# Batched fp32 matmul on one core: all 32 batches in one TensorE loop, the first pair's x loaded in fp32 and rounded on chip

## The chip, the cores and the metric

The kernel runs on one core of one Trainium2 chip. The metric is the device time of one execution in microseconds. The kernel before takes 513.82 us, the median of 3 runs (513.75 to 513.89). A second number comes from one profiled execution, which took 514.01 us and from which all the durations below are read.

## What is computed

For each of 32 batches, out = x @ weight, with x of 512 x 1024, weight of 1024 x 768 and out of 512 x 768, all fp32 in memory. The reference is one line:

```python
return np.matmul(x, weight).astype(np.float32)   # x [32, 512, 1024], weight [32, 1024, 768]
```

The kernels round x and weight to bf16 on the way in and accumulate in fp32.

## The kernel before

Five engines run programs written out by hand, tied together by semaphores; nothing is scheduled by a planner.

**Loads.** GpSimd (POOL, `on_pool`, L309) issues the loads on its own DMA queue, q0 in the profile. These DMAs read fp32 and write bf16, so the rounding costs no engine anything. A batch's weight (3.15 MB in memory) goes to one of four slots `ws` (`load_w`, L89), after the batch that used the slot four batches earlier has been multiplied. x is loaded for two batches in one DMA (`load_x`, L94, 4.19 MB in memory) into one of two slots `xs`, after the transposes of the pair that used the slot. In it partitions 0 to 63 hold the first batch of the pair and 64 to 127 the second, eight rows of 1024 in each partition. Only batch 0's x comes in fp32, by one DMA that SyncE (SP) issues on queue q1 at the very start (L359), into memory that a later output tile uses.

**Pairs.** Batch 0 stands alone, then come 15 pairs (1, 2), (3, 4) to (29, 30), and batch 31 stands alone again. For a pair TensorE (`pair_on_pe`, L159) waits for x, transposes it in 8 groups of 4 instructions (`transpose`, L151), two bf16 numbers travelling as one fp32 word, and then multiplies the two batches, each after a wait for its weight (`take(s_wr)`, L168; the wait itself is L157). VectorE spreads each transposed group from PSUM into `both` (L233). Batch 0 needs 32 transposes for itself because its x is fp32, batch 31 needs 16. Seven turns of a loop hold 14 of the pairs; the rest is written out.

**Results.** ScalarE and VectorE copy the products out of PSUM into `outs` (L265, L268, L279, L281). Outputs are paired as (0, 1), (2, 3) and so on: a tile holds the first batch in partitions 0 to 63 and the second in 64 to 127, so a copy covers 64 partitions. Batches 30 and 31 are the exception: each has a tile of 128 partitions (`one` for batch 30) and copies of 128 partitions (L276, and L265 and L268 in that form).

**Stores.** A pair's 3.15 MB goes out in one DMA (`store`, L107). POOL issues stores 0 to 10 between its loads, and stores 11, 12 and 13 behind the last load. SP first waits in order for every weight to land (`landed`, L304, which passes the news to TensorE), and then issues the first half of batch 30, store 14, the second half of batch 30 and both halves of batch 31 (`store_half`, L111). A half of a batch is 0.79 MB, 128 partitions x 6144 B.

**What orders the work.** Each queue's DMAs start in the order in which they were issued, and POOL and SP each wait at the head of their own list. So a load whose slot is free can stand behind a wait of another load.

Of the kernel before, what the change touches and what calls it, by code (L numbers as in the profile page):

```python
# [12 lines left out]
def kernel(  # L13
# [16 lines left out]
    AHEAD = 3  # L30
    LATE = 4
    HELD = 4
    GROUPS = 2 * MT
    W_SLOTS, X_SLOTS, OUT_SLOTS = 4, 2, 4
    LOOPS = (B - 4) // W_SLOTS
    LOOPED = 2 * LOOPS

# [3 lines left out]
    x_view = x.rearrange("b (mi mo) k -> b mi mo k", mi=P)  # L41
    pair_view = x[1:B - 1].rearrange("(p r) (mi mo) k -> p (r mi) mo k", r=2, mo=2 * MT)
    out_view = out.rearrange("b (mi mo) n -> b mi (mo n)", mi=P)
# [9 lines left out]
    outs = [sbuf(f"out{i}", [P, 2 * ROW], F32) for i in range(OUT_SLOTS)]  # L53
    one = sbuf("one", [P, ROW], F32)
    x_first = outs[3][:, :MT * K].rearrange("p (mo k) -> p mo k", mo=MT)
# [11 lines left out]
    s_first, s_zero, s_ident = sem("s_first"), sem("s_zero"), sem("s_ident")  # L67
# [13 lines left out]
    def pt_done(k):  # L81
        return GROUPS * (k + 2)

    def out_done(b):
        return 2 * (b + 1)
# [8 lines left out]
    def load_x(k):  # L94
        if k >= X_SLOTS:
            pool.wait_ge(s_pt, pt_done(k - X_SLOTS))
        slot = xs[k % X_SLOTS]
        if 2 * k + 1 == B - 1:
            pool.dma_start(out=slot[:, :MT], in_=x_view[B - 1]).then_inc(s_x[k % X_SLOTS], 16)
        else:  # L100
            pool.dma_start(out=slot, in_=pair_view[k]).then_inc(s_x[k % X_SLOTS], 16)  # L101
# [5 lines left out]
    def store(eng, a, sem):  # L107
        copied(eng, out_done(2 * a + 1) - 1)
        eng.dma_start(out=two_view[a], in_=outs[a % OUT_SLOTS]).then_inc(sem, 16)  # L109

    def store_half(b, p):  # L111
        src = one if b == B - 2 else outs[(b // 2) % OUT_SLOTS]
        half = slice(p * N2, (p + 1) * N2)
        copied(sp, 2 * b + p)
        sp.dma_start(out=out_view[b, :, half], in_=src[:, half]).then_inc(s_fin, 16)
# [3 lines left out]
    def stationary(b, mt):  # L119
        if b == 0 or b == B - 1:  # L120
            return both[mt][:, 0].rearrange("p j h i r -> p j (h i) r")
        return both[mt][:, (b - 1) % 2].rearrange("p j h i r -> p j (h i) r")
# [20 lines left out]
    def rows_of(b, g):  # L143

        if b == 0:
            return [x_first[:, g // 2, JT * (g % 2) + i::KT] for i in range(JT)]
        words = xs[(b // 2) % X_SLOTS].bitcast(F32)
        mo = g if b == B - 1 else g // 2 + MT * (g % 2)
        return [words[:, mo, j::JT] for j in range(JT)]

    def transpose(b, g):  # L151
        for i, rows in enumerate(rows_of(b, g)):
            last = pe.transpose(pts[g % 2][:, i, :], rows, ident)  # L153
        last.then_inc(s_pt, 1)
# [4 lines left out]
    def pair_on_pe(k, q):  # L159

        b = 2 * k + 1
        take(s_xr)
        for g in range(GROUPS):
            if GROUPS * q + g > 1:
                pe.wait_ge(s_c, GROUPS * q + g - 1)
            transpose(b, g)
        for r in range(2):
            take(s_wr)  # L168
            for mt in range(MT):
                at = 4 * q + 2 * r + mt // 2  # L170
                if not r:
                    pe.wait_ge(s_c, GROUPS * q + 2 * mt + 2)
                pe.wait_ge(s_a, at + 1 + mt % 2)
                if b + r == B - 2 and mt == MT - 1:
                    pe.wait_ge(s_dp, 2 * (B - 2))
                else:
                    pe.wait_ge(s_d, at + 1 + mt % 2)
                multiply(b + r, mt)

    def on_pe():  # L180
        pe.wait_ge(s_ident, 1)
        pe.wait_ge(s_first, 16)
        for g in range(GROUPS):
            if g > 1:
                pe.wait_ge(s_c, g - 1)
            transpose(0, g)
        pe.wait_ge(s_c, GROUPS).then_inc(s_c, -GROUPS)
        take(s_wr)
        for mt in range(MT):
            multiply(0, mt)  # L190
        with pe.Fori(0, LOOPS):
            for q in range(2):
                pair_on_pe(q, q)
            pe.wait_ge(s_c, 2 * GROUPS).then_inc(s_c, -2 * GROUPS)
            pe.wait_ge(s_a, 9).then_inc(s_a, -8)
            pe.wait_ge(s_d, 9).then_inc(s_d, -8)
        pair_on_pe(LOOPED, 0)
        b = B - 1
        take(s_xr)
        for g in range(MT):  # L200
            pe.wait_ge(s_c, GROUPS + max(g - 1, 0))
            transpose(b, g)
        take(s_wr)
        for mt in range(MT):
            j = 2 * b + mt // 2
            pe.wait_ge(s_c, GROUPS + mt + 1)
            pe.wait_ge(s_ap if mt % 2 else s_a, j - 1 if mt % 2 else 5 + mt // 2)
            pe.wait_ge(s_dp, j - 1)
            multiply(b, mt)
# [3 lines left out]
    def spread_first(g):  # L213
        xT, pt = both[g // 2][:, 0].rearrange("p j h i r -> p j (h i) r"), pts[g % 2]
        for j in range(2):
            last = dve.tensor_copy(  # L216
                xT[:, 2 * (g % 2) + j].rearrange("p (h i) r -> p r h i", h=2),
                pt[:, 2 * j:2 * j + 2].rearrange("p r (i h) -> p r h i", h=2),
            )
        return last  # L220

    def spread_pair(k, g):

        pt = pts[g % 2].bitcast(BF16).rearrange("p j (b i r) -> p j b i r", b=2, r=2)
        tile, half = both[g // 2], g % 2
        if 2 * k + 2 == B - 2:

            rows = tile[:, 1].rearrange("p j h i r -> p j (h i r)").rearrange(
                "p j (m r) -> p j m r", r=2
            )  # L230
            dve.tensor_copy(tile[:, 0, :, half], pt[:, :, 0])  # L231
            return dve.tensor_copy(rows[:, :, half::2, :], pt[:, :, 1])  # L232
        return dve.tensor_copy(tile[:, :, :, half].rearrange("p b j i r -> p j b i r"), pt)  # L233

    def spread_last(g):
        return dve.tensor_copy(  # L236
            both[g][:, 0].rearrange("p j h i r -> p (j h i r)"),
            pts[g % 2].bitcast(BF16).rearrange("p j m -> p (j m)"),
        )

    def slot_free(eng, b):
        a = b // 2
        if a >= OUT_SLOTS and b % 2 == 0 and b < B - 2:
            eng.wait_ge(s_st[a % OUT_SLOTS], 16 * (a // OUT_SLOTS))
        if b == B - 1:
            eng.wait_ge(s_st[a % OUT_SLOTS], 16 * (a // OUT_SLOTS))

    def pieces(b, p, i):

        pm = pms[p][i]  # L250
        if b >= B - 2:
            dst = one if b == B - 2 else outs[(b // 2) % OUT_SLOTS]
            at = p * N2 + 512 * i
            return [(dst[:, at:at + 512], pm)]
# [4 lines left out]
    def out_on_act(b, p):  # L259
        j = 2 * b + p  # L260
        if p == 0:
            slot_free(act, b)
# [7 lines left out]
    def out_on_dve(b, p):  # L270
        j = 2 * b + p
        if p == 0:
            slot_free(dve, b)
        dve.wait_ge(s_mm, 2 * j + 2)
        if b >= B - 2:
            dve.tensor_copy(*pieces(b, p, 1)[0]).then_inc(s_dp, 1)  # L276
            return
# [4 lines left out]

    def on_dve():

        for b in range(B):
            if b == 0 or b % 2:
                spread = {0: spread_first, B - 1: spread_last}.get(b)
                for g in range(MT if b == B - 1 else GROUPS):
                    dve.wait_ge(s_pt, (0 if b == 0 else pt_done(b // 2 - 1)) + g + 1)
                    (spread(g) if spread else spread_pair(b // 2, g)).then_inc(s_c, 1)  # L290
                if b:
                    out_on_dve(b - 1, 1)
            out_on_dve(b, 0)
            if b % 2 or b == B - 1:
                out_on_dve(b, 1)

    def on_act():
        for b in range(B):
            out_on_act(b, 0)
            if b % 2 == 0:  # L300
                landed(act, (s_x, s_xr), b // 2)
            out_on_act(b, 1)

    def landed(eng, what, i):  # L304

        slots, ready = what
        eng.wait_ge(slots[i % len(slots)], 16 * (i // len(slots) + 1)).then_inc(ready, 1)

    def on_pool():  # L309
# [12 lines left out]
        load_x(0)  # L322
        load_w(1)
        load_w(2)
        load_x(1)
        for b in range(B):
            if b % 2 and b + AHEAD + 1 < B:
                load_x((b + AHEAD) // 2)
            a = (b - 5) // 2
            if b % 2 and 0 <= a < B // 2 - 1 - HELD:  # L330
                store(pool, a, s_st[a % OUT_SLOTS])
            if b + AHEAD < B:
                load_w(b + AHEAD)
            if b == B - LATE:
                for a in range(B // 2 - 1 - HELD, B // 2 - 2):
                    store(pool, a, s_st[a % OUT_SLOTS])
# [59 lines left out]
```

## Time and profile before

| What | Value |
|---|---|
| profiled execution | 514.01 us, of which the instructions' span is 512.2 |
| TensorE, busy | 437.9 us; first transpose at 12.41, first matmul at 20.66, last matmul ends 501.3 |
| TensorE granted clock, mean | 0.946 |
| VectorE, ScalarE, busy | 206.8 us, 110.2 us |
| a weight load, from issue to landing | 41.6 us (median of 32) |
| a pair's x, from issue to landing | 30.0 us (median of 15) |
| batch 0's x, from issue to landing | 11.3 us |
| last four half stores, from issue to landing | 9.0 to 13.9 us |

How to read it: the busy time of an engine says how long it worked, not whether it was waited for. The time from issue to landing holds the time for which a transfer stood behind others in its queue. The DMA share of a stretch is the mean busy share of the 16 DMA engines that all queues use; it can come out a little above 1, because packets overlap.

### The profile page before, as it was taken

What the parts mean: (1) busy time and instruction counts of PE and PEld (TensorE: products, weight loads), DVE (VectorE), ACT (ScalarE), POOL (GpSimd) and SP (SyncE); (2) the same over time, 40 slices, a digit from 0 to 9 for tenths busy, and PEclk for the clock granted to TensorE, in tenths of its full rate; (3) what the DMA queues carried; (4) which work ended last, traced back from release to release, by engine and by line L of the source; (5) the groups of instructions that cost most, each with busy time, mean ns of one, the idle gap of its engine ahead of it and who ended that gap; (6) DMA issues with size and microseconds to landing.
All of it is one profiled execution on the core that took longest, in us unless ns stands there. A gap on an engine that the chain in (4) does not pass through costs nothing. (4 is left out here: it accounts for less than half of the span.)

```text
span 512.2 us, 6109 instructions
## 1 busy us (share of the span) xinstructions
PE 437.9 (85%) x2576; PEld 278.8 (54%) x2576; DVE 206.8 (40%) x332; ACT 110.2 (22%) x189; POOL 33.7 (7%) x68
## 2 busy tenths in 40 slices
PE   0899989999795997979989798898969979799991
PEld 0666656666463654636646365464635646456660
DVE  0463543545362352533525245153631615416230
ACT  1013122222211221112221122112122121221210
POOL 3000000101010010100101001010100100100000
PEclk9999999999997998979989899799998989979997
DMA  8999999999999999999999999999999999999996
GB/s 254 214 214 222 222 207 224 213 225 325 220 335 218 240 312 224 333 218 255 297 222 337 218 264 286 219 339 218 288 266 213 341 216 306 250 214 257 432 429 290
DMA packets 9803, 135.40 MB, mean 264 GB/s; under 512 B 1088, under 2 KB 1088, under 8 KB 1600
## 3 DMA queue, kind: packets, MB, share of 16 engines
q0 software_dynamic: 8928, 126.88, 96.3%
q1 hardware_dynamic: 864, 8.39, 4.0%
q8 instruction: 5, 0.08, 0.1%
q14 instruction: 6, 0.05, 0.0%
HBM read 167.77 MB, written 50.33 MB: 426 GB/s over the span
## 5 line engine op out<-in xcount | busy, mean ns | idle before, releaser
L134 PE MATMUL pm<-w,xT 128*128 128x256 bf16 (+1 forms) x2048 | 356.2, 337 | 40.2 <-PEq L157 40.2
L134 PEld LDWEIGHTS pm<-w,xT 128*128 128x128 bf16 x2048 | 205.8, 101 | 186.2 <-issue 61.5
L279 DVE COPY out<-pm 64x512 f32<-64x512 f32 x120 | 82.5, 687 | 198.9 <-PE pm L134 198.1
L265 ACT COPY out<-pm 64x512 f32<-64x512 f32 (+1 forms) x122 | 70.7, 580 | 292.8 <-PE pm L134 292.1
L233 DVE COPY xT<-pt 128x1024 bf16<-128x1024 bf16 x112 | 72.2, 687 | 61.0 <-PE pt L153 61.0
L153 PE MATMUL pt<-ident,x 128*128 128x128 f32 x496 | 80.0, 302 | 10.5 <-DVE xT L233 9.5
L153 PEld LDWEIGHTS pt<-ident,x 128*128 128x128 f32 x496 | 69.2, 209 | 21.8 <-DVE xT L233 17.4
L268 ACT COPY out<-pm 64x512 f32<-64x512 f32 (+1 forms) x62 | 35.8, 578 | 90.0 <-PE pm L134 90.0
L281 DVE COPY out<-pm 64x512 f32<-64x512 f32 x60 | 41.2, 686 | 0.0
L101 POOL DMA_DIRECT2D x<-in_x_dram x15 | 8.0, 532 | 266.6 <-PE pt L153 266.4
L92 POOL DMA_DIRECT2D w<-in_weight_dram x32 | 17.2, 538 | 125.4 <-PE pm L134 124.4
L153 PE MATMUL pt<-ident,out 128*128 128x128 f32 x32 | 6.9, 373 | 12.7 <-DMA out<-in_x_dram 12.4
L153 PEld LDWEIGHTS pt<-ident,out 128*128 128x128 f32 x32 | 5.3, 207 | 14.1 <-issue 12.4
L216 DVE CAST xT<-pt 128x256 bf16<-128x256 f32 x16 | 6.0, 441 | 14.4 <-PE pt L153 14.1
L109 POOL DMA_DIRECT2D out_dram<-out x14 | 7.5, 536 | 1.2 <-DVE out L281 0.7
L231 DVE COPY xT<-pt 128x512 bf16<-128x512 bf16 x8 | 3.4, 420 | 4.1 <-PE pt L153 4.1
L276 DVE COPY out<-pm 128x512 f32<-128x512 f32 x2 | 1.4, 692 | 8.4 <-PE pm L134 8.4
L236 DVE COPY xT<-pt 128x1024 bf16<-128x1024 bf16 x4 | 2.6, 688 | 5.2 <-PE pt L153 5.2
L232 DVE COPY xT<-pt 128x512 bf16<-128x512 bf16 x8 | 3.3, 416 | 0.0
L276 DVE COPY one<-pm 128x512 f32<-128x512 f32 x2 | 1.4, 687 | 3.2 <-PE pm L134 3.2
L265 ACT COPY one<-pm 128x512 f32<-128x512 f32 x2 | 1.2, 585 | 4.0 <-PE pm L134 4.0
L268 ACT COPY one<-pm 128x512 f32<-128x512 f32 x2 | 1.2, 586 | 4.0 <-PE pm L134 4.0
(8 smaller groups left out, 2.7 us busy)
## 6 DMA issues: line engine op xcount, KB each, us to landing
w<-in_weight_dram POOLq DMA_DIRECT2D x32, 1536.0 KB, 41.6
out_dram<-out POOLq DMA_DIRECT2D x14, 3072.0 KB, 36.9
x<-in_x_dram POOLq DMA_DIRECT2D x15, 2048.0 KB, 30.0
out_dram<-out SPq DMA_DIRECT2D x1, 3072.0 KB, 19.9
out<-in_x_dram SPq DMA_DIRECT2D x1, 2048.0 KB, 11.3
out_dram<-one SPq DMA_DIRECT2D x2, 768.0 KB, 13.4
out_dram<-out SPq DMA_DIRECT2D x2, 768.0 KB, 10.0
x<-in_x_dram POOLq DMA_DIRECT2D x1, 1024.0 KB, 25.3
```

The lines of the kernel that those rows point to most:

```text
L92: pool.dma_start(out=ws[b % W_SLOTS], in_=w_view[b]).then_inc(s_w[b % W_SLOTS], 16)
L101: pool.dma_start(out=slot, in_=pair_view[k]).then_inc(s_x[k % X_SLOTS], 16)
L109: eng.dma_start(out=two_view[a], in_=outs[a % OUT_SLOTS]).then_inc(sem, 16)
L134: last = pe.matmul(pm[bank][:, at:at + size], xT[:, ko // 2, :, ko % 2], w[:, ko, off:off + size], start=(ko == 0), stop=(ko == KT - 1),)
L153: last = pe.transpose(pts[g % 2][:, i, :], rows, ident)
L216: last = dve.tensor_copy(xT[:, 2 * (g % 2) + j].rearrange("p (h i) r -> p r h i", h=2), pt[:, 2 * j:2 * j + 2].rearrange("p r (i h) -> p r ...
L231: dve.tensor_copy(tile[:, 0, :, half], pt[:, :, 0])
L233: return dve.tensor_copy(tile[:, :, :, half].rearrange("p b j i r -> p j b i r"), pt)
L265: last = act.copy(*piece)
L268: act.copy(*pieces(b, p, 2)[0]).then_inc(s_ap, 1)
L279: last = dve.tensor_copy(*piece)
L281: dve.tensor_copy(*pieces(b, p, 2)[1]).then_inc(s_dp, 1)
```

## The change

The pairs become (0, 1), (2, 3) to (30, 31), for x as they already were for out. TensorE's whole program is one loop of eight turns with two pairs each; the separate code for batch 0 and batch 31, the tile `one` and the spreads in two parts go away.

The x of the first pair is loaded in fp32 by SP into memory of output tiles 2 and 3 (32 KB in each partition). VectorE rounds four of its eight rows into the first x slot and ScalarE the other four, ScalarE's last one after all of VectorE's; then ScalarE tells TensorE that x is ready. POOL's list at the start becomes weights 0 and 1, x of the second pair, weights 2 and 3. After that its order in a pair is as before: x of two pairs ahead, a store, two weights. The weights are now those of the batches that use the slots just freed by this pair's own two batches. Stores 0 to 11 stand between the loads, 12 and 13 behind them.

The last pair's output tile is in the pair layout, too. SP issues store 14 first and then four halves: the first two come out of partitions 0 to 63 (batch 30), the last two out of partitions 64 to 127 (batch 31), each as two pieces of 6144 B in a partition.

```diff
-    LOOPS = (B - 4) // W_SLOTS
+    LOOPS = B // W_SLOTS
...
-    x_view = x.rearrange("b (mi mo) k -> b mi mo k", mi=P)
-    pair_view = x[1:B - 1].rearrange("(p r) (mi mo) k -> p (r mi) mo k", r=2, mo=2 * MT)
-    out_view = out.rearrange("b (mi mo) n -> b mi (mo n)", mi=P)
+    x_view = x.rearrange("(p r) (mi mo) k -> p (r mi) mo k", r=2, mo=2 * MT)
...
-    x_first = outs[3][:, :MT * K].rearrange("p (mo k) -> p mo k", mo=MT)
+    x_first = all_outs[:, 4 * ROW:4 * ROW + 2 * MT * K].rearrange("p (mo k) -> p mo k", mo=2 * MT)
...
     def store_half(b, p):
-        src = one if b == B - 2 else outs[(b // 2) % OUT_SLOTS]
+        a, r = divmod(b, 2)
+        rows = slice(H * r, H * (r + 1))
         half = slice(p * N2, (p + 1) * N2)
+        src, dst = (
+            t[rows].rearrange("i (h c) -> i h c", h=2)[:, :, half]
+            for t in (outs[a % OUT_SLOTS], two_view[a])
+        )
         copied(sp, 2 * b + p)
-        sp.dma_start(out=out_view[b, :, half], in_=src[:, half]).then_inc(s_fin, 16)
+        sp.dma_start(out=dst, in_=src).then_inc(s_fin, 16)
...
     def on_pe():
         pe.wait_ge(s_ident, 1)
...
         with pe.Fori(0, LOOPS):
-            for q in range(2):
-                pair_on_pe(q, q)
...
-        pair_on_pe(LOOPED, 0)
...
+            for k in range(2):
+                pair_on_pe(k)
...
+    def cast_first(eng, copy, rows):
+
+        eng.wait_ge(s_first, 16)
+        for mo in rows:
+            if mo == 2 * MT - 1:
+                eng.wait_ge(s_cast, 1)
+            last = copy(xs[0][:, mo], x_first[:, mo])
+        return last
+
     def on_dve():
...
+        dve.sem_inc(s_d, 2)
+        cast_first(dve, dve.tensor_copy, range(MT)).then_inc(s_cast, 1)
...
     def on_act():
+        act.sem_inc(s_a, 2)
+        cast_first(act, act.copy, range(MT, 2 * MT)).then_inc(s_xr, 1)
...
-        load_x(0)
         load_w(1)
+        load_x(1)
         load_w(2)
-        load_x(1)
...
+        load_w(3)
+        for k in range(PAIRS - 2):
+            load_x(k + 2)
+            if k >= 2:
+                store(pool, k - 2, s_st[(k - 2) % OUT_SLOTS])
+            load_w(2 * k + 4)
+            load_w(2 * k + 5)
+        for a in range(PAIRS - 2 - HELD, PAIRS - 2):
+            store(pool, a, s_st[a % OUT_SLOTS])
...
-        store_half(B - 2, 0)
-        store(sp, B // 2 - 2, s_fin)
-        store_half(B - 2, 1)
-        store_half(B - 1, 0)
-        store_half(B - 1, 1)
+        store(sp, PAIRS - 2, s_fin)
+        for b in (B - 2, B - 1):
+            for p in range(2):
+                store_half(b, p)
```

More of the change, by code (lines that the diff above doesn't have):

```diff
@@ L29 @@
     ROW = MT * N
-    AHEAD = 3
-    LATE = 4
-    HELD = 4
+    PAIRS = B // 2
+    HELD = 2
     GROUPS = 2 * MT
     W_SLOTS, X_SLOTS, OUT_SLOTS = 4, 2, 4
-    LOOPS = (B - 4) // W_SLOTS
-    LOOPED = 2 * LOOPS
+    LOOPS = B // W_SLOTS
     pe, dve, act, pool, sp = nc.tensor, nc.vector, nc.scalar, nc.gpsimd, nc.sync
     w_view = weight.rearrange("b (ki ko) n -> b ki ko n", ki=P)
-    x_view = x.rearrange("b (mi mo) k -> b mi mo k", mi=P)
-    pair_view = x[1:B - 1].rearrange("(p r) (mi mo) k -> p (r mi) mo k", r=2, mo=2 * MT)
-    out_view = out.rearrange("b (mi mo) n -> b mi (mo n)", mi=P)
+    x_view = x.rearrange("(p r) (mi mo) k -> p (r mi) mo k", r=2, mo=2 * MT)
     two_view = out.rearrange("(p r) (i m) n -> p (r i) (m n)", r=2, m=2 * MT)
@@ L52 @@
     both = [sbuf(f"xT{i}", [P, 2, JT, 2, H, 2], BF16) for i in range(MT)]
-    outs = [sbuf(f"out{i}", [P, 2 * ROW], F32) for i in range(OUT_SLOTS)]
-    one = sbuf("one", [P, ROW], F32)
-    x_first = outs[3][:, :MT * K].rearrange("p (mo k) -> p mo k", mo=MT)
+    all_outs = sbuf("outs", [P, OUT_SLOTS * 2 * ROW], F32)
+    outs = [all_outs[:, i * 2 * ROW:(i + 1) * 2 * ROW] for i in range(OUT_SLOTS)]
+    x_first = all_outs[:, 4 * ROW:4 * ROW + 2 * MT * K].rearrange("p (mo k) -> p mo k", mo=2 * MT)
     pts = [nc.alloc_psum_tensor(f"pt{i}", [P, JT, P], F32).ap() for i in range(2)]
@@ L65, in sem @@
         return sems[-1]
-    s_first, s_zero, s_ident = sem("s_first"), sem("s_zero"), sem("s_ident")
+    s_first, s_cast, s_zero, s_ident = (sem(f"s_{n}") for n in ("first", "cast", "zero", "ident"))
     s_w = [sem(f"s_w{i}") for i in range(W_SLOTS)]
@@ L81, in pt_done @@
     def pt_done(k):
-        return GROUPS * (k + 2)
-    def out_done(b):
-        return 2 * (b + 1)
+        return GROUPS * (k + 1)
     def load_w(b):
@@ L96, in load_x @@
             pool.wait_ge(s_pt, pt_done(k - X_SLOTS))
[L97 to L101, printed above, removed]
+        pool.dma_start(out=xs[k % X_SLOTS], in_=x_view[k]).then_inc(s_x[k % X_SLOTS], 16)
     def copied(eng, j):
@@ L107, in store @@
     def store(eng, a, sem):
-        copied(eng, out_done(2 * a + 1) - 1)
+        copied(eng, 4 * a + 3)
         eng.dma_start(out=two_view[a], in_=outs[a % OUT_SLOTS]).then_inc(sem, 16)
     def store_half(b, p):
-        src = one if b == B - 2 else outs[(b // 2) % OUT_SLOTS]
+        a, r = divmod(b, 2)
+        rows = slice(H * r, H * (r + 1))
         half = slice(p * N2, (p + 1) * N2)
+        src, dst = (
+            t[rows].rearrange("i (h c) -> i h c", h=2)[:, :, half]
+            for t in (outs[a % OUT_SLOTS], two_view[a])
+        )
         copied(sp, 2 * b + p)
-        sp.dma_start(out=out_view[b, :, half], in_=src[:, half]).then_inc(s_fin, 16)
+        sp.dma_start(out=dst, in_=src).then_inc(s_fin, 16)
     def stationary(b, mt):
-        if b == 0 or b == B - 1:
-            return both[mt][:, 0].rearrange("p j h i r -> p j (h i) r")
-        return both[mt][:, (b - 1) % 2].rearrange("p j h i r -> p j (h i) r")
+        return both[mt][:, b % 2].rearrange("p j h i r -> p j (h i) r")
     SPLITS = (
@@ L141, in multiply, with transpose @@
         last.then_inc(s_mm, 1)
[L143 to L153, printed above, removed]
+    def transpose(k, g):
+        words = xs[k % X_SLOTS].bitcast(F32)
+        mo = g // 2 + MT * (g % 2)
+        for j in range(JT):
+            last = pe.transpose(pts[g % 2][:, j, :], words[:, mo, j::JT], ident)
         last.then_inc(s_pt, 1)
@@ L157, in take, with await_copies, pair_on_pe @@
         pe.wait_ge(s, 1).then_inc(s, -1)
-    def pair_on_pe(k, q):
-        b = 2 * k + 1
+    def await_copies(s, n, last, step):
+        wait = pe.wait_ge(s, n)
+        if n == last:
+            wait.then_inc(s, -step)
+    def pair_on_pe(k):
         take(s_xr)
         for g in range(GROUPS):
[L164 to L167, printed above, removed]
+            if GROUPS * k + g > 1:
+                pe.wait_ge(s_c, GROUPS * k + g - 1)
+            transpose(k, g)
+        for b in (2 * k, 2 * k + 1):
@@ L168, in pair_on_pe @@
             take(s_wr)
             for mt in range(MT):
[L170 to L178, printed above, removed]
+                if b % 2 == 0:
+                    await_copies(s_c, GROUPS * k + 2 * mt + 2, 2 * GROUPS, 2 * GROUPS)
@@ L180, in on_pe @@
+                at = 2 * b + mt // 2 + 1 + mt % 2
+                await_copies(s_a, at, 9, 8)
+                await_copies(s_d, at, 9, 8)
+                multiply(b, mt)
     def on_pe():
         pe.wait_ge(s_ident, 1)
[L182 to L190, printed above, removed]
@@ L191, in on_pe @@
-        with pe.Fori(0, LOOPS):
-            for q in range(2):
-                pair_on_pe(q, q)
-            pe.wait_ge(s_c, 2 * GROUPS).then_inc(s_c, -2 * GROUPS)
-            pe.wait_ge(s_a, 9).then_inc(s_a, -8)
-            pe.wait_ge(s_d, 9).then_inc(s_d, -8)
-        pair_on_pe(LOOPED, 0)
[L198 to L209, printed above, removed]
@@ L213, in spread_first @@
[L213 to L222, printed above, removed]
-        pt = pts[g % 2].bitcast(BF16).rearrange("p j (b i r) -> p j b i r", b=2, r=2)
[L225 to L245, printed above, removed]
+        with pe.Fori(0, LOOPS):
+            for k in range(2):
+                pair_on_pe(k)
+    def spread(k, g):
+        pt = pts[g % 2].bitcast(BF16).rearrange("p j (b i r) -> p j b i r", b=2, r=2)
+        to = both[g // 2][:, :, :, g % 2].rearrange("p b j i r -> p j b i r")
+        return dve.tensor_copy(to, pt)
@@ L246, in slot_free @@
+    def slot_free(eng, a):
+        if a >= OUT_SLOTS:
             eng.wait_ge(s_st[a % OUT_SLOTS], 16 * (a // OUT_SLOTS))
@@ L250, in pieces @@
         pm = pms[p][i]
[L251 to L254, printed above, removed]
         mine = outs[(b // 2) % OUT_SLOTS][H * (b % 2):H * (b % 2 + 1)]
@@ L260, in out_on_act @@
         j = 2 * b + p
-        if p == 0:
-            slot_free(act, b)
+        if b % 2 == 0 and p == 0:
+            slot_free(act, b // 2)
         act.wait_ge(s_mm, 2 * j + 1)
@@ L271, in out_on_dve @@
         j = 2 * b + p
-        if p == 0:
-            slot_free(dve, b)
+        if b % 2 == 0 and p == 0:
+            slot_free(dve, b // 2)
         dve.wait_ge(s_mm, 2 * j + 2)
-        if b >= B - 2:
-            dve.tensor_copy(*pieces(b, p, 1)[0]).then_inc(s_dp, 1)
-            return
         for piece in pieces(b, p, 1):
@@ L281, in out_on_dve, with landed @@
         dve.tensor_copy(*pieces(b, p, 2)[1]).then_inc(s_dp, 1)
-    def on_dve():
[L285 to L295, printed above, removed]
+    def cast_first(eng, copy, rows):
[5 more added lines that the diff above has]
+        return last
+    def on_dve():
+        dve.sem_inc(s_d, 2)
+        cast_first(dve, dve.tensor_copy, range(MT)).then_inc(s_cast, 1)
+        for k in range(PAIRS):
+            for g in range(GROUPS):
+                dve.wait_ge(s_pt, GROUPS * k + g + 1)
+                spread(k, g).then_inc(s_c, 1)
+            for j in range(4 * k - 1, 4 * k + 3):
+                if j >= 0:
+                    out_on_dve(*divmod(j, 2))
+        out_on_dve(B - 1, 1)
     def on_act():
+        act.sem_inc(s_a, 2)
+        cast_first(act, act.copy, range(MT, 2 * MT)).then_inc(s_xr, 1)
         for b in range(B):
             out_on_act(b, 0)
-            if b % 2 == 0:
-                landed(act, (s_x, s_xr), b // 2)
+            if b % 2 and b < B - 1:
+                landed(act, s_x, s_xr, b // 2 + 1, (b // 2 + 2) // 2)
             out_on_act(b, 1)
-    def landed(eng, what, i):
-        slots, ready = what
-        eng.wait_ge(slots[i % len(slots)], 16 * (i // len(slots) + 1)).then_inc(ready, 1)
+    def landed(eng, slots, ready, i, n):
+        eng.wait_ge(slots[i % len(slots)], 16 * n).then_inc(ready, 1)
     def on_pool():
@@ L321, in on_pool @@
         ).then_inc(s_ident, 1)
-        load_x(0)
         load_w(1)
+        load_x(1)
         load_w(2)
-        load_x(1)
[L326 to L336, printed above, removed]
+        load_w(3)
[7 more added lines that the diff above has]
+            store(pool, a, s_st[a % OUT_SLOTS])
     def on_sp():
         for b in range(B):
-            landed(sp, (s_w, s_wr), b)
-        store_half(B - 2, 0)
-        store(sp, B // 2 - 2, s_fin)
-        store_half(B - 2, 1)
-        store_half(B - 1, 0)
-        store_half(B - 1, 1)
+            landed(sp, s_w, s_wr, b, b // W_SLOTS + 1)
+        store(sp, PAIRS - 2, s_fin)
+        for b in (B - 2, B - 1):
+            for p in range(2):
+                store_half(b, p)
         sp.sem_inc(s_zero, 1)
@@ L351, in clear_on_pool @@
         for i, s in enumerate(s_st):
-            pool.wait_ge(s, 16 * len(range(i, B // 2 - 2, OUT_SLOTS)))
+            pool.wait_ge(s, 16 * len(range(i, PAIRS - 2, OUT_SLOTS)))
         pool.wait_ge(s_zero, 2)
```

## The prediction

> **What bounds the kernel now.** I read the tenths of the span first, because the shares in part 1 average over stages.
>
> ```profile
> PE 437.9 (85%) x2576; PEld 278.8 (54%) x2576; DVE 206.8 (40%) x332; ACT 110.2 (22%) x189; POOL 33.7 (7%) x68
> ...
> DMA  8999999999999999999999999999999999999996
> ...
> q0 software_dynamic: 8928, 126.88, 96.3%
> q1 hardware_dynamic: 864, 8.39, 4.0%
> ...
> HBM read 167.77 MB, written 50.33 MB: 426 GB/s over the span
> ```
>
> TensorE looks busiest, but the DMA row has a 9 in every slice except the first and the last, and the two data queues together fill 100.3% of 16 engines' span. The GB/s row counts what lands in SBUF, so a load that rounds counts half; the HBM line counts all bytes. Next I asked what TensorE waits for, and what the DMA does at the end, in stretches of 2 us (the last three columns are granted clock, DMA share, GB/s):
>
> ```profile
> PE pm L134 <- PEq L157: 40.2, 13, 5.2
> ```
>
> ```profile
> 484.00:486.00 2.00, 2.00 (x15) 1.22 (x13) 0.00 (x0) 0.28 (x1) 0.00 (x0) 1.00 1.06 455
> ...
> 502.00:504.00 2.00, 0.00 (x0) 0.00 (x0) 0.01 (x1) 0.00 (x0) 0.00 (x0) 1.00 0.93 390
> 504.00:506.00 2.00, 0.00 (x0) 0.00 (x0) 0.00 (x0) 0.00 (x0) 0.00 (x0) 0.77 1.00 418
> 506.00:508.00 2.00, 0.00 (x0) 0.00 (x0) 0.00 (x0) 0.00 (x0) 0.00 (x0) 0.50 0.91 381
> 508.00:510.00 2.00, 0.00 (x0) 0.00 (x0) 0.00 (x0) 0.00 (x0) 0.00 (x0) 0.50 0.29 123
> 510.00:512.00 2.00, 0.00 (x0) 0.00 (x0) 0.00 (x0) 0.00 (x0) 0.00 (x0) 0.50 0.04 15
> ```
>
> L157 is the wait for loaded weights: 13 times, 40.2 us. After TensorE's last matmul (501.3) the DMA goes on at full share until about 508 and trails off over 3 us. So the page's chain (TensorE from 448 to 501) names the last engine, but the last transfers are held by a backlog of transfers. The steady pairs say the same: POOL issues a pair of x at 118.15 and ten pairs later at 434.72, 31.66 us a pair, for 4.19 MB of x, 6.29 MB of weight and 3.15 MB of stores (13.63 MB, 430 GB/s). TensorE's own work for a pair is 5.66 us of transposes (85.56 to 91.22) and 20.96 of matmul, 26.6 us. **The DMA engines set the time from 2 us to 508 us.** An edit counts only if it changes their work, leaves them idle, or slows them.
>
> **The change, part by part,** against the profiled execution's 514.01 us (span 512.2, 1.8 around it; the median is 513.82, so 0.2 less).
>
> Bytes. x, weight and out are moved once in both kernels: 218.1 MB. What differs is form. Before, the first batch's x is 128 fp32 packets (16 KB) on q1 and the last batch's is 128 rounded ones on q0. By the trace's DMA records an fp32 packet takes 0.624 us (mean 0.728, the first being slow) and a rounded one 0.625: over 16 engines 5.8 + 5.0 = 10.8 us. After, the first pair's x is 4.19 MB of fp32: 8 x 2 x 0.624 = 10.0, or with 0.728 11.7. So -0.8 to +0.9 us; I take 0.
>
> The start. x of batch 0 landed 11.3 us after its issue. Twice the bytes take at least 5.0 us more (16.3), and at most 5.0/0.4 = 12.5 more (23.8), 0.4 being q1's share in the records of 8 to 11 us. I take 17, since longer packets win a larger share: x at 18. Then four rounding copies of 1024 columns on each of VectorE and ScalarE, which before doesn't show. Bounds for one on VectorE: 0.69 us (L233, 1024 bf16 columns) and 4 x 0.441 (L216, 256 fp32 columns), so 2.7 to 7.1 for four; on ScalarE one or two of the 0.58 copies (L265), 2.3 to 4.7. ScalarE's last one waits for VectorE's four, and nothing is queued behind either that could run earlier. With that row added, 3 to 8 us; I take 4.3. TensorE starts its first transposes at 22.3, not 12.4, and its first matmul at 27.9, not 20.7. After three batches and two transpose stages it stands at 27.9 + 20.96 + 5.66 + 10.4 = 64.9, where before it was at 57.5: **7.4 us late**, 18 at the far bounds. What hides it: TensorE needs 26.6 us for a pair and the DMA 31.7, so the 40.2 us of waits shrink first. It counts only if the DMA engines run dry behind it. POOL's loads of batches 4 to 7 now wait for the batch four before. The load of batch 5 is issued when batch 1 is done, 48.9 (far bound 59.4), when the queue holds 28.3 MB from 2 us on, work until 68.6 at 425 GB/s. The load of batch 7 is issued at 75.4 (86) with work until 93. Seven us remain in the worst case, so the cost is 0; with that cover gone it would be the excess itself.
>
> [...]
>
> The loop. Loads keep their order on POOL (x, store, two weights), but the weight slot freed by a pair's second batch is refilled at once instead of after the next transposes (about 6 us sooner). That deepens the queue and cannot raise a full rate: 0. The stall moves from a pair's second batch to its first. The last batch's 16 transposes go (2.6 us, 488.1 to 490.7), and the spreads in two parts: TensorE and VectorE, under the DMA: 0.
>
> The end. Store 11 now stands ahead of the last two weights on POOL's queue. Batch 31's weight landed at 474.6 in before; 3.15 MB more ahead makes it 482.0, and batch 30's 474.6. SP's own stores come behind its wait for that landing, as before. TensorE: batch 30 from 474.6, 10.4 us or 13.33 as after the stall at 448.22; batch 31 ends at 495 to 498. The last copies are in 64-partition form, on VectorE three of 0.69 instead of one (+1.4), so the last half is issued by 500.5 (502.1 before). Behind the weights stand stores 12, 13, 14 and four halves, 12.58 MB or 29.6 us: 511.6. The same sum for before, 474.6 + 15.73 MB, gives 511.6 too, and its last store landed at 511.1. So this part alone is 0, with 11 us between the last issue and the end of the queue as cover.
>
> What is left is **how the halves are read**. Before, each of the four is 128 partitions x 6144 B. Now batch 30 lies in partitions 0 to 63 and batch 31 in 64 to 127 (L102 to L109 of after): 64 partitions x 2 pieces of 6144 B. No row shows a DMA of 64 partitions. From below: the packets keep their size and 0.234 us, cost 0. From above: 128 partitions are needed for the full rate and half of them give half, four halves of 8 packets per engine, 32 x 0.234 = 7.5 us more. What speaks for the upper end is that all kinds of packet run at one rate for an engine (24,576 B stores in 0.912 us, 6,144 B in 0.234, 16 KB of fp32 in 0.624: 26.9, 26.3, 26.3 GB/s), as if the path into SBUF were the limit, not HBM or the kind of work; and the nearest row with half the partitions, the copies, is no faster for it:
>
> ```profile
> L279 DVE COPY out<-pm 64x512 f32<-64x512 f32 x120 | 82.5, 687 | 198.9 <-PE pm L134 198.1
> ...
> L276 DVE COPY out<-pm 128x512 f32<-128x512 f32 x2 | 1.4, 692 | 8.4 <-PE pm L134 8.4
> ```
>
> Half the data, the same time: half the rate. I go by that. Packets that alternate with those of stores 12 and 13 may escape. In the records of 488 to 494 (shares 0.80 and 0.20) one small packet goes beside each whole store's packet. Store 14 would start about 485 (3 us after its issue, like the first half of before, issued 483.9 and first seen at 487.4), alternate one to one with stores 12 and 13, and be through 14.6 us later at 499.6; then store 13 has some 5 packets of an engine left, beside which 5 small ones go. So 27 of 32 pay: 27 x 0.234 = **+6.4 us**. Nothing covers it: the DMA runs alone from 501.
>
> [...]
>
> Sum: 514.0 + 0 + 0 + 6.4 = 520.4, against the median 520.2.
>
> **Rivals.**
> *Halves at full rate: not slower.* The engines may be what limits a packet (26 GB/s in each kind fits that as well), and the last halves run beside each other's tails. Then everything above is 0: 514.0, with -1 to +1 for the form of the first x and the trailing 3 us. This decides if a 6144 B packet from 64 partitions stays near 0.234 us. Chance 0.24.
> *A shorter tail: faster.* DMA shares of 0.29 and 0.04 in the last 4 us are 3.3 us of engines waiting for the slowest one. If the new split evens them out, up to 2 us go: 512.3. Against it: the same count of equal packets. Chance 0.08.
> *The late start runs the DMA dry.* If x comes still later than my far bound, loads 4 to 7 start late and the gap stays to the end: some 4 us beyond the cover, with the halves as forecast 524.4, alone 518. Against it: at least 7 us of queue. Chance 0.07.
> *The forecast:* 0.61, its own range 516.5 to 522.
>
> **How the numbers follow.** The likeliest case is 520.2. The range reaches from the full-rate case (513 less the form of x, 512.8) to all 32 packets paying and the form's +0.9 (522.3). It leaves out the rest of the tail case and the dry start. What a measurement here can tell from no change is 0.2%, 1.03 us. Slower: 0.61 + 0.07 + 0.02 of the full-rate case = 0.70. Same: 0.20 of that case. Faster: 0.08 + 0.02 = 0.10.
>
> **What will show it.** DMA share at 9 tenths between slices 2 and 39; first transposes at 20 to 30 us; one wait for weights per pair, before its first batch; a last matmul before 501 while SP's last store lands 8 to 12 us behind it. The halves' rate decides: in the last 8 us a GB/s near 210 with the forecast, near 420 with its rival. I am wrong if the DMA row falls below 9 between 40 and 100 us, or if the last half is issued after 505.

## The result, and the profile after

The changed kernel takes 519.18 us, the median of 5 runs (518.55 to 519.64), against 513.82 (513.02 to 514.16). The ratio is 1.0104, with a 95% interval of 1.0089 to 1.0119. The profiled execution took 518.67 us, its span 516.9. The page first:

```profile
span 516.9 us, 6028 instructions
...
DMA  8999999999999999999999999999999999999995
GB/s 294 259 217 223 207 222 213 215 323 229 225 326 220 333 218 255 297 221 336 217 280 273 220 335 215 309 247 215 338 219 324 224 241 313 223 333 217 422 397 163
...
q0 software_dynamic: 8784, 125.83, 94.5%
q1 hardware_dynamic: 864, 10.49, 5.5%
...
HBM read 167.77 MB, written 50.33 MB: 422 GB/s over the span
```

The DMA row is as full as before, and the bytes are the same. The two queues again add up to 100% of the engines' span, of a span that is 4.7 us longer. (Packets overlap: the share of 506 to 508 below is 1.03. So a sum of 100% does not mean that no engine was ever idle.) The last number of the GB/s row stands out, 163, where the row of the kernel before ends with 290. The waits of TensorE come next:

```profile
PE pm L126 <- PEq L144: 26.5, 8, 5.5
PE pt L140 <- PEq L144: 22.7, 1, 22.7
```

TensorE starts 10 us later (22.7 instead of 12.4) and waits less for weights, 8 times in place of 13. It ends earlier. The last copy is over at 499.25 and the last half is issued at 499.32, where it was 502.1 before. So TensorE does not set the end. The end in stretches of 2 us (last columns: clock, DMA share, GB/s):

```profile
498.00:500.00 2.00, 0.00 (x0) 0.00 (x0) 1.24 (x2) 0.00 (x0) 0.00 (x0) 0.92 0.96 412
500.00:502.00 2.00, 0.00 (x0) 0.00 (x0) 0.00 (x0) 0.00 (x0) 0.00 (x0) 0.50 0.97 350
502.00:504.00 2.00, 0.00 (x0) 0.00 (x0) 0.00 (x0) 0.00 (x0) 0.00 (x0) 0.50 1.00 292
504.00:506.00 2.00, 0.00 (x0) 0.00 (x0) 0.00 (x0) 0.00 (x0) 0.00 (x0) 0.50 0.96 316
506.00:508.00 2.00, 0.00 (x0) 0.00 (x0) 0.00 (x0) 0.00 (x0) 0.00 (x0) 0.50 1.03 298
508.00:510.00 2.00, 0.00 (x0) 0.00 (x0) 0.00 (x0) 0.00 (x0) 0.00 (x0) 0.50 0.75 200
510.00:512.00 2.00, 0.00 (x0) 0.00 (x0) 0.00 (x0) 0.00 (x0) 0.00 (x0) 0.50 0.57 160
512.00:514.00 2.00, 0.00 (x0) 0.00 (x0) 0.00 (x0) 0.00 (x0) 0.00 (x0) 0.50 0.24 58
514.00:516.00 2.00, 0.00 (x0) 0.00 (x0) 0.00 (x0) 0.00 (x0) 0.00 (x0) 0.50 0.06 15
```

From 500 to 508 the engines are as busy as ever and move 290 to 350 GB/s. The kernel before moved 402 there:

```profile
500.00:508.00 8.00, 1.28 (x8) 0.51 (x6) 0.69 (x1) 0.58 (x1) 0.00 (x0) 0.82 0.95 402
508.00:516.00 8.00, 0.00 (x0) 0.00 (x0) 0.00 (x0) 0.00 (x0) 0.00 (x0) 0.61 0.08 35
```

After 508 they trail off for 7 us instead of 3. So a share of 0.97 to 1.03 says here that packets are under way, not that they run at full rate. In the trace's DMA records the 512 packets of 6144 B, all at 0.234 us before, now come in two kinds: 313 near 0.234 us and 199 of over 0.3, most of them near 0.46, twice as long. Their mean is 0.329.

### The profile page after: what moved, and what is told of

The parts are those of the page before. It is cut to its first block, busy times and chain, and to the rows that moved or that the text cites. A ratio compares the mean times of both kernels' runs of the same rounds, so it can differ in the third digit from the quotient of the medians.

```text
span 516.9 us, 6028 instructions
## 1 busy us (share of the span) xinstructions
PE 430.2 (83%) x2512; PEld 277.4 (54%) x2560; DVE 212.4 (41%) x324; ACT 116.4 (23%) x197; POOL 33.2 (6%) x67
## 5 line engine op out<-in xcount | busy, mean ns | idle before, releaser
L126 PE MATMUL pm<-w,xT 128*128 128x256 bf16 (+1 forms) x2000 | 349.1, 335 | 34.1 <-PEq L144 26.5
L212 DVE COPY outs<-pm 64x512 f32<-64x512 f32 x128 | 88.1, 688 | 198.1 <-PE pm L126 196.8
L201 ACT COPY outs<-pm 64x512 f32<-64x512 f32 x128 | 74.2, 580 | 272.6 <-PE pm L126 271.8
L140 PE MATMUL pt<-ident,x 128*128 128x128 f32 x512 | 84.5, 309 | 32.9 <-PEq L144 22.7
L182 DVE COPY xT<-pt 128x1024 bf16<-128x1024 bf16 x128 | 82.9, 687 | 70.0 <-PE pt L140 70.0
L140 PEld LDWEIGHTS pt<-ident,x 128*128 128x128 f32 x512 | 72.7, 209 | 45.1 <-issue 22.7
L204 ACT COPY outs<-pm 64x512 f32<-64x512 f32 x64 | 37.0, 578 | 91.4 <-PE pm L126 91.4
L214 DVE COPY outs<-pm 64x512 f32<-64x512 f32 x64 | 43.9, 686 | 0.0
L222 DVE CAST x<-outs 128x1024 bf16<-128x1024 f32 x4 | 2.5, 688 | 18.7 <-DMA outs<-in_x_dram 18.7
L98 POOL DMA_DIRECT2D out_dram<-outs x14 | 7.5, 537 | 7.8 <-DVE outs L214 7.6
L222 ACT CAST x<-outs 128x1024 bf16<-128x1024 f32 x4 | 3.9, 1041 | 16.4 <-DMA outs<-in_x_dram 16.4
## 6 DMA issues: line engine op xcount, KB each, us to landing
outs<-in_x_dram SPq DMA_DIRECT2D x1, 4096.0 KB, 17.7
```

Of the source, the lines that this page charges most:

```text
L126: last = pe.matmul(pm[bank][:, at:at + size], xT[:, ko // 2, :, ko % 2], w[:, ko, off:off + size], start=(ko == 0), stop=(ko == KT - 1),)
L140: last = pe.transpose(pts[g % 2][:, j, :], words[:, mo, j::JT], ident)
L182: return dve.tensor_copy(to, pt)
L201: last = act.copy(*piece)
L204: act.copy(*pieces(b, p, 2)[0]).then_inc(s_ap, 1)
L212: last = dve.tensor_copy(*piece)
```

## The experiments

The theory: it matters *which* partitions a half store reads; from 0 to 63, or from 64 to 127, many of its packets take about 0.46 us in place of 0.234. The rivals: the late start and the new order at the end cost the time; the *number* of partitions counts, whichever they are; the pattern of two pieces in a partition is slow in itself. Every ratio below is to the kernel before, on the same chip.

**Halves of 128 partitions.**

```diff
-        a, r = divmod(b, 2)
-        rows = slice(H * r, H * (r + 1))
...
-        src, dst = (
...
+        src, dst = outs[(B // 2 - 2) % OUT_SLOTS][:, half], out_view[b, :, half]
```

> The changed kernel, but its four last half stores read 128 partitions x 6144 B, as before the change. They read the tile of pair 14, which is complete by then, so the output of the last two batches is pair 14's: the instant of each issue, the bytes and everything ahead of it stay. Theory 'half the partitions': the 5.4 us go, 513.5 to 514.5, and all 512 packets of 6144 B take 0.234 us. Rival 'start and order': the loss comes from the late first pair or from store 14 and the halves standing all behind the last weight; then it stays at 518.5 to 519.7 and the packets still take 0.234.

Measured: 514.09 us, ratio 1.0008 (0.9998 to 1.0018). All packets take 0.234 us. With its halves at 128 partitions the changed kernel takes what the kernel before takes. The rival "start and order" falls: everything else in the change is worth about 0.4 us by the ratio (0.9 at the end of its interval).

**64 partitions in the middle.**

```diff
-            t[rows].rearrange("i (h c) -> i h c", h=2)[:, :, half]
-            for t in (outs[a % OUT_SLOTS], two_view[a])
...
+        src = outs[(a - 1) % OUT_SLOTS][32:96].rearrange("i (h c) -> i h c", h=2)[:, :, half]
+        dst = two_view[a][rows].rearrange("i (h c) -> i h c", h=2)[:, :, half]
```

> The changed kernel, but each half store reads partitions 32 to 95 of pair 14's tile: still 64 partitions x 2 pieces of 6144 B, written to the same rows of out (with pair 14's numbers). [...] Rival 'how many partitions' (a path belongs to each partition, 64 are half): 518.5 to 519.7, packets at 0.33 in the mean. Rival 'two pieces per partition' (the pattern itself is slow): 518.5 to 519.7 too, but then the run with 128 partitions is fast.

If it matters which partitions are read, I expected 513.5 to 514.5 us and packets at 0.234. Measured: 514.15 us, ratio 1.0010 (1.0001 to 1.0020), all packets at 0.234 us. The number of partitions, the two pieces and the rows of out are those of the changed kernel; only the partitions differ, and the 5 us are gone. The end of this run, and then that of the changed kernel, in two stretches:

```profile
500.00:508.00 8.00, 0.00 (x0) 0.00 (x0) 0.00 (x0) 0.00 (x0) 0.00 (x0) 0.61 0.95 399
508.00:516.00 8.00, 0.00 (x0) 0.00 (x0) 0.00 (x0) 0.00 (x0) 0.00 (x0) 0.60 0.07 31
```

```profile
500.00:508.00 8.00, 0.00 (x0) 0.00 (x0) 0.00 (x0) 0.00 (x0) 0.00 (x0) 0.50 0.99 314
508.00:516.00 8.00, 0.00 (x0) 0.00 (x0) 0.00 (x0) 0.00 (x0) 0.00 (x0) 0.50 0.40 108
```

The DMA share is slightly lower with the middle rows (0.95 against 0.99), yet the rate is a quarter higher (399 against 314). Both other rivals fall.

**All four halves from partitions 0 to 63.**

```diff
-            t[rows].rearrange("i (h c) -> i h c", h=2)[:, :, half]
-            for t in (outs[a % OUT_SLOTS], two_view[a])
...
+        src = outs[(a - 1) % OUT_SLOTS][:H].rearrange("i (h c) -> i h c", h=2)[:, :, half]
+        dst = two_view[a][rows].rearrange("i (h c) -> i h c", h=2)[:, :, half]
```

> The changed kernel, but all four half stores read partitions 0 to 63 (of pair 14's tile; batch 30 and 31 get pair 14's numbers). In the changed kernel batch 30 is read from 0 to 63 and batch 31 from 64 to 127, so DMA engines that have got to batch 31 leave the others alone. Theory 'which partitions': no such escape, more packets at 0.46 us, 520 to 523 us. Rival 'how many partitions' and rival 'start and order': the same as the changed kernel, 518.5 to 519.7.

Measured: 519.66 us, ratio 1.0123 (1.0106 to 1.0140). That is below the 520 I expected, and its interval overlaps that of the changed kernel (1.0089 to 1.0119), so the time does not settle it. The packets do:

```profile
500.00:508.00 8.00, 0.00 (x0) 0.00 (x0) 0.00 (x0) 0.00 (x0) 0.00 (x0) 0.60 0.97 270
508.00:516.00 8.00, 0.00 (x0) 0.00 (x0) 0.00 (x0) 0.00 (x0) 0.00 (x0) 0.50 0.66 157
```

The rate from 500 to 508 is 270 GB/s in place of 314, and near 210 from 506 to 510; 332 of 512 packets take over 0.3 us instead of 199, their mean is 0.386. With all halves in partitions 0 to 63 fewer packets escape, that is, stay at 0.234 us. It shows best from 504 on, when the last whole store is through: 289 of 347 small packets take over 0.3 us here, 151 of 341 in the changed kernel (44 of the 161 that start before batch 30's halves have landed at 507.1, 107 of the 180 behind that). The time grows little: the slow packets add 4.9 us to an engine in the mean, where they added 3.0, but the trail at the end is shorter, since the share stays at 0.90 or more until 512.

**The kernel before, with the halves of the changed one.**

```diff
-        src = one if b == B - 2 else outs[(b // 2) % OUT_SLOTS]
+        a, r = divmod(b, 2)
+        rows = slice(H * r, H * (r + 1))
         half = slice(p * N2, (p + 1) * N2)
+        src, dst = (
+            t[rows].rearrange("i (h c) -> i h c", h=2)[:, :, half]
+            for t in (outs[(a - 1) % OUT_SLOTS], two_view[a])
+        )
...
-        sp.dma_start(out=out_view[b, :, half], in_=src[:, half]).then_inc(s_fin, 16)
+        sp.dma_start(out=dst, in_=src).then_inc(s_fin, 16)
```

> The kernel before, with nothing changed but its four half stores: they read 64 partitions x 2 pieces of 6144 B of pair 14's tile (0 to 63 for batch 30, 64 to 127 for batch 31 by the same view; here 0 to 63 or 64 to 127 as the changed kernel does), issued at the same instants as before; the last two batches get pair 14's numbers. Theory 'half the partitions': 516.5 to 519.5, the first half beside stores 12 and 13 nearly free. Rival 'start and order': 513.5 to 514.5.

Measured: 521.93 us, ratio 1.0159 (1.0142 to 1.0176). The part alone does it, without any of the other edits, but it costs 8 us, not 3 to 6. I had thought that the first half, beside stores 12 and 13, would be nearly free. Most of its own packets do escape: 20 of 128 take over 0.3 us. But the *whole* stores beside the halves got slower. From 488 to 498, 28 of 129 of their packets take over 1 us (1 of 145 in the kernel before). Store 14's packets of 24,576 B take 1.027 us in the mean and up to 2.133 (0.913 and 0.954 in the kernel before), and store 14 lands 24.4 us after its issue, where it landed after 19.9. This run, and then the kernel before:

```profile
out_dram<-out SPq DMA_DIRECT2D x4, 768.0 KB, 17.8
out_dram<-out SPq DMA_DIRECT2D x1, 3072.0 KB, 24.4
```

```profile
out_dram<-out SPq DMA_DIRECT2D x1, 3072.0 KB, 19.9
```

**The same with the middle partitions.** Source as in the second run, in the kernel before.

```diff
-        src = one if b == B - 2 else outs[(b // 2) % OUT_SLOTS]
...
+        src = outs[(a - 1) % OUT_SLOTS][32:96].rearrange("i (h c) -> i h c", h=2)[:, :, half]
+        dst = two_view[a][rows].rearrange("i (h c) -> i h c", h=2)[:, :, half]
```

> The kernel before with its four half stores from partitions 32 to 95 of pair 14's tile (two pieces of 6144 B; the last two batches get pair 14's numbers), the counterpart of the run that had the kernel before with halves from 0 to 63 and 64 to 127 and took 521.93. Theory 'which partitions': 513.3 to 514.5, no packet of any store slower than before. Rival (in this order of stores the two-piece pattern or the number of partitions is what cost 8 us): 517 to 522.

Measured: 513.66 us, ratio 0.9997 (0.9988 to 1.0007). In the kernel before, too, all 8 us belong to which partitions are read. Why they cost 8 there and 5 in the changed kernel, the records show for the most part. In the mean over the engines the slow small packets add 3.9 us there (3.0 in the changed kernel), and the slower whole stores 1.7 (0.1 in the changed kernel, where only the last packets of store 13 have halves beside them). That is 2.6 of the 3 us; the rest is the trail.

**Two joint stores for the last pair.** Each half of the columns leaves for both batches at once, from all 128 partitions.

```diff
...
-            t[rows].rearrange("i (h c) -> i h c", h=2)[:, :, half]
+            t.rearrange("i (h c) -> i h c", h=2)[:, :, half]
...
-        for b in (B - 2, B - 1):
-            for p in range(2):
-                store_half(b, p)
+        for p in range(2):
+            store_half(p)
...
```

> The changed kernel, but the last pair leaves in two stores instead of four: each holds one column half of both batches, 128 partitions x 2 pieces of 6144 B, issued when batch 31's copies of that half are done. Every number is stored as the reference has it. Theory 'which partitions': 513.5 to 514.5, as the kernel before, because all 128 partitions are read and stores 12, 13 and 14 keep the DMA busy until about 503, when both are long issued. A rival by which fewer and later issues leave the DMA idle: 515 to 517, with a DMA share below 0.9 before 505. It beats the kernel before only if the last transfers trail less than 3 us.

Measured: 514.06 us, ratio 1.0004 (0.9995 to 1.0013). The first of the two is issued at 495.0, the second at 500.2, and the DMA never waits for them:

```profile
500.00:502.00 2.00, 0.00 (x0) 0.00 (x0) 0.16 (x1) 0.00 (x0) 0.00 (x0) 1.00 0.92 384
502.00:504.00 2.00, 0.00 (x0) 0.00 (x0) 0.00 (x0) 0.00 (x0) 0.00 (x0) 0.66 0.98 412
504.00:506.00 2.00, 0.00 (x0) 0.00 (x0) 0.00 (x0) 0.00 (x0) 0.00 (x0) 0.50 0.99 415
506.00:508.00 2.00, 0.00 (x0) 0.00 (x0) 0.00 (x0) 0.00 (x0) 0.00 (x0) 0.50 0.91 381
508.00:510.00 2.00, 0.00 (x0) 0.00 (x0) 0.00 (x0) 0.00 (x0) 0.00 (x0) 0.50 0.24 98
```

This keeps the single loop and the pairs and loses nothing against the kernel before. It does not beat it, since the last 3 us trail as before.

**The first pair's x rounded by POOL's queue,** on top of the joint stores.

```diff
+        load_x(0)
         load_w(0)
...
-        cast_first(dve, dve.tensor_copy, range(MT)).then_inc(s_cast, 1)
...
-        cast_first(act, act.copy, range(MT, 2 * MT)).then_inc(s_xr, 1)
+        landed(act, s_x, s_xr, 0, 1)
```

> As the run with two joint stores, but the first pair's x comes rounded by POOL's queue, first in its list, and VectorE and ScalarE round nothing. Theory (the start is hidden behind the DMA, and fp32 packets cost what rounded ones do): within 1 us of the run with two joint stores. Rival 'the late start costs': the first transposes come 6 to 10 us sooner and the time falls by 1 us or more.

Measured: 514.98 us, ratio 1.0025 (1.0016 to 1.0034): 0.9 us slower, although the first transposes come 8.6 us sooner (14.2). The late start of TensorE costs nothing here. The DMA's first microseconds account for the 0.9. First the run with joint stores, then this one:

```profile
1.00:2.00 1.00, 0.00 (x0) 0.00 (x0) 0.00 (x0) 1.00 (x1) 0.52 (x1) 1.00 0.50 131
```

```profile
1.00:2.00 1.00, 0.00 (x0) 0.00 (x0) 0.00 (x0) 0.00 (x0) 0.52 (x1) 1.00 0.00 0
```

SP's first packet starts at 1.98 us, and POOL's queue, which has to begin the work in this run, has its first at 2.86.

**A start that is later still,** on top of the joint stores.

```diff
     def on_act():
         act.sem_inc(s_a, 2)
+        for n in range(4):
+            cast_first(act, act.copy, range(MT, 2 * MT)).then_inc(s_rep, 1)
+            act.wait_ge(s_rep, n + 1)
         cast_first(act, act.copy, range(MT, 2 * MT)).then_inc(s_xr, 1)
```

> As the run with two joint stores, but ScalarE rounds its four rows five times over, one pass after another, so that the first transposes come some 16 us later, at about 39. Theory (a queue of loads covers the start): POOL's loads of batches 4 to 7 still find work ahead of them, or miss it by at most 2 us: 513.5 to 517. Rival 'a late start is paid in full': 528 to 531.

Measured: 517.82 us, ratio 1.0078 (1.0063 to 1.0094). The first transposes come at 38.5, 15.8 us later than in the changed kernel, and 3.8 us of that are paid, so that the time lies above the 513.5 to 517 that I expected. The cover is there, but it is thinner than I reckoned. The DMA engines run dry for a moment, twice:

```profile
68.00:72.00 4.00, 3.62 (x25) 3.11 (x25) 3.27 (x6) 0.00 (x0) 0.00 (x0) 1.00 0.91 169
...
92.00:96.00 4.00, 3.51 (x24) 2.81 (x23) 2.31 (x4) 0.58 (x1) 0.53 (x1) 1.00 0.77 134
```

POOL issues the load of batch 5 at 66.8 and that of batch 7 at 93.2. My sum in the prediction had the queue's work end at 68.6 and at 93, and that is where the share falls. What the sum lacked is the time between an issue and a full stream of packets: after the issue at 93.2 the share is back to 1 only at 96. What is lost so early stays lost: against the run with joint stores, batch 5's weight lands 2.0 us later (79.2), and the x of the pair (8, 9), behind batch 7's weight, 2.5 us later (114.6). The delay grows to 3.4 us at batch 31's weight (486.0), and for this last part I have no cause.

## Why the prediction was right, step by step

**DMA-bound from 2 us on: right.** With the halves undone (514.09) and with joint stores (514.06) all the rest of the change costs 0.2 to 0.4 us by the ratios, and TensorE's work, 16 transposes less and a new place for the stalls, shows nowhere in the time. The stall did move to a pair's first batch.

**The form of the first x, taken as 0: right.** Its 128 packets of 32 KB took 1.319 us each, 10.6 us over the engines, where I set 10.0 to 11.7 against 10.8 before. What I missed is that having SP begin the DMA's work is worth 0.9 us (514.98 against 514.06); the kernel before has it as well.

**The start: right, with a cover that was smaller than stated.** x landed 17.7 us after its issue (17 taken), the rounding took 2.5 us on VectorE and 3.9 on ScalarE (4.3 taken for both), the transposes began at 22.73 (22.3). These lines give the rounding:

```profile
L222 DVE CAST x<-outs 128x1024 bf16<-128x1024 f32 x4 | 2.5, 688 | 18.7 <-DMA outs<-in_x_dram 18.7
...
L222 ACT CAST x<-outs 128x1024 bf16<-128x1024 f32 x4 | 3.9, 1041 | 16.4 <-DMA outs<-in_x_dram 16.4
```

The first matmul came at 29.88, not 27.9, because the first 32 transposes took 7.3 us instead of 5.66. After three batches TensorE stood at 66.8, 9.3 us late rather than 7.4. It cost nothing. The step "seven us remain in the worst case", at 18 us late, would leave about 0 at the 25 us of the last experiment. There 3.8 us were lost, so the cover was some 4 us thinner than I made it. The bytes were right, as the two dry moments show; I had let a load count from its issue, not from its packets, which explains 2 to 3 us of it; the rest stays open.

**The end of the loads and of TensorE: right.** Batch 30's and 31's weights landed at 474.2 and 481.5 (474.6 and 482.0 forecast), store 14's packets ran from 485.2 to 499.0 (485 to 499.6), the last half was issued at 499.3 (500.5).

**The halves: they cost what I said they might, but not for the reason I went by.** I had reasoned that 128 partitions are needed for the full rate, so that half of them give half, and took the copies of 64 partitions on VectorE as the nearest row. No run shows it, and the runs with partitions 32 to 95 (514.15 and 513.66 us) refute it: 64 partitions there take 0.234 us a packet, like 128. What costs is that the halves lie in 0 to 63 and in 64 to 127, where 199 of 512 packets take over 0.3 us. That the changed kernel's halves lie just there, so that the term came out near, was luck as far as my reason goes.

The size was partly luck, too. +6.4 us stood for 27 of 32 packets at twice 0.234 (6.3, to be exact). The difference to the same kernel with 128-partition halves is 519.18 - 514.09 = 5.1 us (4.9 by the ratios). It is made up otherwise. Not 27 of 32 packets are slow but 199 of 512, about 12 of 32, and the mean packet takes 0.329, not 0.43: 32 x 0.095 = 3.0 us in the mean over the engines. The remaining 2 us or so are the longer trail, for which my sum had nothing. That some engines met more slow packets than others would explain it; the records do not name the engine, so this is not shown.

Two things were wrong in the choice of 27. Packets away from whole stores do not all pay: from 504 on 151 of 341 do with the halves in 0 to 63 and 64 to 127, and 289 of 347 did with all of them in 0 to 63. And packets beside whole stores do not escape for nothing: with the kernel before's order the halves slow the whole stores down (store 14's packets from 0.913 to 1.027 us). Of the signs that I had named, two did not come: the rate was not near 210 but 290 to 350 from 500 to 508, with 108 in the mean of the 8 us behind that, and SP's last store landed some 18 us behind the last matmul (515.8 and 497.2), not 8 to 12.

**The rivals.** "Halves at full rate" is what the kernel with other partitions does (514.15 us), not this one. A shorter tail did not come about: it is longer. The dry start needs a start later by more than the change has.

## What to carry to other kernels

Where the DMA engines set the time, look past their busy share to the rate: here the share stayed at 0.97 to 0.99 while the rate fell from 400 to between 270 and 314 GB/s. A store of 64 partitions is no slower for being 64 (514.15 us from 32 to 95, 514.09 from all 128); it matters which they are (519.18 from 0 to 63 and 64 to 127; only stores were tried here), so store a pair by columns from all 128 partitions, or lay the 64 in 32 to 95. An engine's late start is free only as long as the load queue holds work (15.8 us more cost 3.8 here), and that can be read ahead from what is issued and when the next slot falls free, with 2 to 3 us taken off for the time until a load's packets run (93.2 to 96 here).

## What the runs showed of the hardware that I had not expected

Packets from partitions 0 to 63 or 64 to 127 come mainly in two durations, 0.234 and about 0.46 us, rather than one in between: in the changed kernel 305 of 512 take less than 0.25 us and 163 take 0.44 to 0.52. Both occur in batch 31's halves (64 to 127) alone, too: of the 180 packets that start after batch 30's halves have landed (507.1), 107 take over 0.3 us. The records kept here do not name the DMA engine, so why a packet takes the one time or the other is not shown. And such transfers slow others: store 14 with its 128 partitions, beside them in the kernel before, went from 0.913 to 1.027 us a packet, one of them to 2.133.
